# Splitting attention-projection weights one chunk ahead, and both ScalarE writes of a turned head pair first

## The chip, the cores and the metric

The kernel runs on one core of a Trainium2 chip. The metric is the device time of one execution in microseconds (us): the median of several runs. Beside the runs there is one profiled execution, whose trace shows every instruction. The engines are TensorE (PE, with its weight loads PEld), VectorE (DVE), ScalarE (ACT), GpSimd (POOL) and the sync engine (SP), which here only issues transfers.

## The reference

Two layers of an encoder on a sequence of 512 positions with 1024 channels. Each layer is a half-step feed-forward block, a mixer, and another half-step feed-forward block, all with an RMS norm and an adaptive shift, scale and gate in front. The change touches only the mixer, and of it the projections to the queries, keys and values of two attentions:

```python
def hybrid_mixer(h, w_in, qk_gain, rel_bias, forget_bias, w_pool, pool_scale, w_branch, w_out):
    proj = h @ w_in
    qa, ka, va, ub, qc, kc, vc, f_lin, g_lin = jnp.split(proj, SPLIT_POINTS, axis=-1)
    ya = chunked_relpos_attention(ha(qa), ha(ka), ha(va), qk_gain[0], qk_gain[1], rel_bias)
    yb = multiscale_pool(ub, w_pool, pool_scale)
    yc = forgetting_attention(hc(qc), hc(kc), hc(vc), qk_gain[2], qk_gain[3], f_lin + forget_bias)
    ...
    branch = jnp.einsum('bsnw,nwd->bsnd', ys, w_branch)
    gates = jax.nn.sigmoid(g_lin.reshape(B, S, N_BRANCHES, D_MODEL))
    merged = jnp.sum(gates * branch, axis=2)
    return merged @ w_out
```

Both attentions have 8 heads of 64 channels. Their queries and keys are RMS-normed per head and scaled by a gain; logits get a bias, then softmax, then the product with the values.

## The kernel before

All products keep close to fp32 precision by a split: a number x becomes hi, its value in the rounded type fp32r, and lo = x - hi. A product of x and y is then three TensorE products, hi by hi, hi by lo and lo by hi. `triple` (lines 137 to 142) issues these three; its lines 139 to 141 are where most of TensorE's time stands.

**Weight chunks.** `wchunk` (lines 296 to 312) brings in 128x1024 weights: a transfer on the sync queue into a tile `raw` (line 300; two places), a ScalarE copy that rounds it to hi (line 309), and a VectorE subtraction that makes lo (line 311). hi and lo lie in one place of the tag `w`, of which there are three. A chunk can be brought in when a place of `raw` and one of `w` are free, that is when VectorE has made the lo of the second chunk before, and TensorE has done the products of the chunk that held the place.

**Projections.** Queries, keys and values of the two attentions are six columns of 512 channels, numbered 0 to 5 (`col`). `proj` (lines 780 to 819) makes one column for all 512 positions, in four accumulators `acc` of 128 positions each. Its weights come in four chunks c = 0 to 3 of 256 input rows. Chunks 0 and 1 are used one after the other: bring it in, then 8 triples over 2 row blocks (`kk`) and 4 position blocks (`t`). Chunks 2 and 3 are then brought in together and held, and each `t` in turn gets its last 4 triples and is evacuated. Column 0 of a layer has its own path, with its first three chunks brought in during the phase before. `proj` is a generator: it gives way after each triple.

For queries and keys (`proj_qk`, lines 838 to 906) the evacuation copies the accumulator (line 846), squares it on ScalarE (line 848) and sums per head on VectorE (line 849). Later come eight small steps for the norm, and four **turns** (lines 869 to 889). A turn takes a pair of heads: four TensorE transposes into one PSUM tile `pt` (line 872), and then, for each of the two heads, which lie in partitions 0 to 63 and 64 to 127:

- a ScalarE write of the scaled, rounded half (line 881);
- for queries a transfer, issued by GpSimd, that copies it to the other half of the partitions (line 884), and a GpSimd memset (line 885);
- a VectorE step that computes the remainder lo (line 887).

**Where they run.** `Mixer.run` (lines 1171 to 1260) first makes columns 0 and 1, the forget gates (`forget`, lines 921 to 952) and column 2. Then comes `attention` of group a (lines 984 to 1074) on columns 0 to 2. For each head and each block of 128 positions it issues the logits (lines 995, 996), the minimum of the negated logits on VectorE (line 999), the exponential on ScalarE (line 1003), and the division by the sum on GpSimd or VectorE (line 1007). The blocks' transposes (line 1019) with their split (lines 1023, 1024), and the product with the values (lines 1041 to 1048), come later, by a list of tasks with due times counted in TensorE work (`later`, `poll`; one unit is a product of 512 columns, and LAG_T = 30 units lie between a block's logits and its transposes). Between the blocks a filler generator gets 9 units of products each. The filler of group a is columns 3, 4 and 5 (`fill_a`, lines 1187 to 1190); that of group c is the gates and branch products of the merge.

**Order.** The code lists the instructions, but it doesn't fix their order on an engine: the program is laid out at build time by readiness, in which earlier code goes first among what is ready, and by explicit rules where the code gives one. On the chip every engine works through its own list in that order.

Of the kernel before, what the change touches and what calls it, by code (L numbers as in the profile page):

```python
# [18 lines left out]
AF = mybir.ActivationFunctionType  # L19
# [21 lines left out]
def encoder_kernel(tc, xT, c, w_ada, b_ada, gains, w_gate, w_up, w_down, w_qkv, w_f, w_ubg,  # L41
                   qk_gain, rel, fbias, w_pool, pool_scale, w_branch, w_out, inv_cnt, w_first, out):
    nc = tc.nc
# [252 lines left out]
    def wchunk(src, shape, side=True, spare=None, lo_eng=None, place=WIDE):  # L296
        lo_eng = lo_eng or nc.vector
        side_work(side)
        raw = st([P] + list(shape), F32, *(("b", NB) if spare else ("raw", NRAW)))
        last["dma"] = nc.sync.dma_start(raw, src).ins  # L300
        if spare == "ptb":
            hi, lo = duo(shape, "ptb")
        elif spare == "b":
            hi = st([P] + list(shape), F32R, "b", NB)
            lo = st([P] + list(shape), F32R, "b", NB)
        else:
            hi, lo = duo(shape, "w", place)
        with behind("scalar"):
            nc.scalar.copy(hi, raw)  # L309
        with behind("vector"):  # L310
            lo_eng.tensor_tensor(lo, raw, hi.bitcast(F32), op=ALU.subtract)  # L311
        return hi, lo
# [463 lines left out]
    def qkv_chunk(l, col, c, **kw):  # L776
        return wchunk(w_qkv[l, 2 * c * P:(2 * c + 2) * P, col * T:(col + 1) * T]
                      .rearrange("(k p) c -> p k c", p=P), (2, T), **kw)

    def proj(l, col, evac, pre=None, norm=None):  # L780
        accs = [acc() for _ in range(NT)]

        def three(t, k, hi, lo):
            tk = slice(t * P, (t + 1) * P)
            triple2(accs[t], hhi[:, k, tk], hlo[:, k, tk], hi, lo, k == 0, k == KD - 1)

        if norm is not None:
            for hs in range(2):
                norm.back(hs, mmt)
                if hs == 0:  # L790
                    later(FRONT2, lambda: norm.front(1, mmt))
                    later(BACK2, lambda: norm.back(1, mmt))
                both = (2 * hs, 2 * hs + 1)
                for k in range(6):
                    hi, lo = pre[k // 2]
                    for t in both:
                        three(t, k, hi[:, k % 2, :], lo[:, k % 2, :])
                if hs == 0:
                    rest = qkv_chunk(l, col, 3)
                for t in both:  # L800
                    for kk in range(2):
                        three(t, 6 + kk, rest[0][:, kk, :], rest[1][:, kk, :])
                    evac(t, accs[t])
                yield
            return
        else:
            for c in range(2):
                hi, lo = qkv_chunk(l, col, c)
                for kk in range(2):
                    for t in range(NT):  # L810
                        three(t, 2 * c + kk, hi[:, kk, :], lo[:, kk, :])
                        yield
        held = [(c, *qkv_chunk(l, col, c)) for c in (2, 3)]
        for t in range(NT):
            for c, hi, lo in held:
                for kk in range(2):
                    three(t, 2 * c + kk, hi[:, kk, :], lo[:, kk, :])
                    yield
            evac(t, accs[t])

    def triple2(o, lh, ll, rh, rl, start, stop):
        triple(o, lh, ll, rh, rl, start, stop)
# [15 lines left out]
    def proj_qk(l, col, gcol, is_q, res, pre=None, norm=None):  # L838
        lows = []
        qs = []  # L840

        def evac(t, a):
            if t == 0:
                qs.extend((st([P, NT, T], F32, "ptb", 2), st([P, NT, H], F32, "qss", 1)))
            qn, ss = qs
            nc.scalar.copy(qn[:, t, :], a)
            sq = t2(T)
            nc.scalar.activation(sq, a, AF.Square)  # L848
            nc.vector.tensor_reduce(ss[:, t, :], sq.rearrange("p (h d) -> p h d", h=H), axis=AX.X, op=ALU.add)

        yield from proj(l, col, evac, pre, norm)
        qn, ss = qs
        norm_of = {}

        def first():
            v = st([P, NT * H], F32, "nt_v32", 2)
            nc.vector.tensor_scalar(v, ss.rearrange("p t h -> p (t h)"), 1.0 / HD, EPS, op0=ALU.mult, op1=ALU.add)
            norm_of["steps"] = rsqrt_steps(v, NT * H)
            next(norm_of["steps"])

        def step():
            norm_of["r"] = next(norm_of["steps"])

        def scale(t):
            q3 = qn[:, t, :].rearrange("p (h d) -> p h d", h=H)
            r = norm_of["r"][:, t * H:(t + 1) * H].unsqueeze(2).to_broadcast([P, H, HD])
            nc.vector.tensor_tensor(q3, q3, r, op=ALU.mult)

        def turn(p):
            pt = mmt()  # L870
            for t in range(NT):
                nc.tensor.transpose(pt[:, t * P:(t + 1) * P], qn[:, t, p * P:(p + 1) * P], ident)
            pe[0] += 2.2
            b = blk("b")
            if is_q:
                lows.append(blk("b"))
            first, second = slice(0, HD), slice(HD, P)
            for odd, (own, other) in enumerate(((first, second), (second, first))):
                dst = b[:, odd, :]
                gc = gcol[own, :]  # L880
                nc.scalar.activation(dst[own, :], pt[own, :], AF.Identity, scale=gc)
                low = dst[other, :]
                if is_q:
                    nc.gpsimd.dma_start(low.bitcast(F32), dst[own, :].bitcast(F32))
                    nc.gpsimd.memset(lows[p][other, odd, :].bitcast(F32), 0.0)
                    low = lows[p][own, odd, :]
                nc.vector.scalar_tensor_tensor(low, pt[own, :], gc, dst[own, :].bitcast(F32),
                                               op0=ALU.mult, op1=ALU.subtract)
            res.append((b, lows[p]) if is_q else b)

        todo = [first, step, step, step] + [lambda t=t: scale(t) for t in range(NT)]
        todo += [lambda p=p: turn(p) for p in range(4)]
        turns.append(todo)
        for n in range(8):
            later(PACE * n, lambda n=n: todo.pop(0)() if len(todo) == 12 - n else None)

        def ready(p):
            if len(todo) >= 4 - p:
                if heads[0] < (Q_GATE if is_q else K_GATE)[p]:
                    later(8, lambda: ready(p))  # L900
                else:
                    while len(todo) >= 4 - p:
                        todo.pop(0)()

        for p in range(4):
            later(TURN + 12 * p, lambda p=p: ready(p))
# [423 lines left out]
```

## Time and profile before

| | |
|---|---|
| runs, median (lowest to highest) | 2371.16 us (2369.97 to 2371.98) |
| the profiled execution | 2367.45 us |
| its span, first to last instruction | 2365.7 us |
| TensorE clock granted | 1.000 of full speed |
| DMA, mean over the span | 137 GB/s |

The span is one execution's; a sum of terms is made against it and then carried over to the median. "Idle before" is the time in which an engine had nothing running before an instruction, and the releaser is what ended it, read from the semaphores. Matmuls overlap, so a busy TensorE is one that always had the next product ready, and its idle time is what other engines cost it.

### The profile page before, as it was taken

The page shows a single profiled execution, that of the slowest core. Times are in us where ns is not written, and L with a number is a line of the kernel's source. Part 1 is how long each engine was busy: PE and PEld are TensorE (multiplying, and loading weights), DVE is VectorE, ACT ScalarE, POOL GpSimd, SP SyncE. Part 2 cuts the span into 40 slices and gives each one's busy share as a digit, 9 for nine tenths or more (in the row PEclk, how much of TensorE's full clock was granted, in tenths as well). Part 3 has the DMA queues.
Part 4 walks back from the last instruction along what each step waited for, and adds up shares of the span by engine and source line. Part 5 has one row for each costly group of instructions (what it writes and reads, how often), then busy time and mean ns, then how long its engine had stood idle before and what let it go on. Part 6 is the DMA issues. An engine that isn't in the chain of part 4 may idle for free.

```text
span 2365.7 us, 37435 instructions
## 1 busy us (share of the span) xinstructions
PE 2336.6 (99%) x14322; PEld 2077.1 (88%) x14322; DVE 1771.6 (75%) x3147; ACT 1198.3 (51%) x2097; POOL 325.8 (14%) x433
## 2 busy tenths in 40 slices
PE   7999999999999999999999999999999999999999
PEld 5898998878888898989999989978888888999898
DVE  8887866787686577878687878677866855878583
ACT  5353555676632363635553536456765324636262
POOL 3000011244411110000100000112443211000000
PEclk9999999999999999999999999999999999999999
DMA  8535342333355524353425353533333654143333
GB/s 294 180 107 187 101 167 88 106 98 110 120 196 208 187 72 160 115 181 106 152 63 178 99 186 108 187 107 99 98 122 106 216 205 167 63 143 108 100 99 105
DMA packets 117976, 325.16 MB, mean 137 GB/s; under 512 B 11651, under 2 KB 13827, under 8 KB 117797
## 3 DMA queue, kind: packets, MB, share of 16 engines
q1 hardware_dynamic: 115106, 314.38, 40.1%
q0 software_dynamic: 2688, 8.39, 1.2%
q8 instruction: 112, 1.84, 0.3%
q14 instruction: 68, 0.55, 0.1%
q10 hardware_dynamic: 2, 0.00, 0.0%
HBM read 312.16 MB, written 6.38 MB: 135 GB/s over the span
## 4 chain that ended last, share of the span: by engine, by line
PE 89%; DVE 6%; ACT 2%; DMA 1%; issue 1%; POOL 0%; SPq 0%; ACTq 0%; DVEq 0%; POOLq 0%
PE acc L139 16%; PE acc L141 16%; PE acc L140 16%; PE acc L148 5%; PE mm L149 5%; PE mm L150 5%; PE mm L148 5%; PE acc L149 5%; PE acc L150 5%; PE mm L141 3%; PE mm L139 3%; PE mm L140 3%; PE mm L1019 1%; DVE v L226 1%; DVE w L311 1%
## 5 line engine op out<-in xcount | busy, mean ns | idle before, releaser
L311 DVE TENSOR_TENSOR w<-raw,w 128x1024 fp32r<-128x1024 f32 x247 | 313.0, 1271 | 163.8 <-ACT w L309 163.6
L309 ACT CAST w<-raw 128x1024 fp32r<-128x1024 f32 (+1 forms) x255 | 264.4, 1041 | 275.5 <-PE acc L141 191.4
L139 PE MATMUL acc<-b,w 128*128 128x512 f32 (+1 forms) x960 | 359.8, 375 | 0.0
L141 PE MATMUL acc<-b,w 128*128 128x512 f32 (+1 forms) x960 | 356.3, 371 | 0.0
L140 PE MATMUL acc<-b,w 128*128 128x512 f32 (+1 forms) x960 | 356.3, 371 | 0.0
L141 PEld LDWEIGHTS acc<-b,w 128*128 128x128 f32 x960 | 180.3, 188 | 31.8
L139 PEld LDWEIGHTS acc<-b,w 128*128 128x128 f32 x960 | 180.3, 188 | 30.1
L140 PEld LDWEIGHTS acc<-b,w 128*128 128x128 f32 x960 | 180.4, 188 | 29.8
L416 ACT CAST ptb<-v 128x1024 fp32r<-128x1024 f32 x140 | 147.0, 1053 | 97.1 <-DVE v L485 58.2
L417 DVE TENSOR_TENSOR ptb<-v,ptb 128x1024 fp32r<-128x1024 f32 x140 | 170.8, 1223 | 32.6 <-ACT ptb L416 27.6
L139 PE MATMUL acc<-hhi,w 128*128 128x512 f32 x480 | 191.8, 401 | 2.6 <-ACT hhi L746 1.7
L141 PE MATMUL acc<-hhi,w 128*128 128x512 f32 x480 | 188.4, 393 | 1.8 <-DVE w L311 1.8
L140 PE MATMUL acc<-hlo,w 128*128 128x512 f32 x480 | 188.2, 392 | 1.1 <-DVE hlo L749 1.1
L416 ACT CAST w<-raw 128x1024 fp32r<-128x1024 f32 (+1 forms) x140 | 116.5, 832 | 120.7 <-PE acc L141 56.0
L417 DVE TENSOR_TENSOR w<-raw,w 128x1024 fp32r<-128x1024 f32 (+1 forms) x140 | 133.4, 953 | 13.2 <-ACT w L416 13.2
L139 PE MATMUL acc<-w,hhi 128*128 128x512 f32 x336 | 138.8, 414 | 0.8 <-ACT t L848 0.8
L140 PE MATMUL acc<-w,hhi 128*128 128x512 f32 x336 | 131.7, 392 | 0.0
L141 PE MATMUL acc<-w,hlo 128*128 128x512 f32 x336 | 131.7, 392 | 0.0
L226 DVE CUSTOM_DVE_ANT_0 v<-v,b,badac 128x1024 f32<-128x1024 f32 x87 | 116.7, 1351 | 11.6 <-DMA v<-in_w_ada_dram 11.3
L466 DVE SCALAR_TENSOR_TENSOR xv<-acc,badac,xv 128x512 f32<-128x512 f32 (+1 forms) x112 | 77.4, 691 | 54.8 <-PE acc L141 54.7
L148 PE MATMUL acc<-b,ptb 128*128 128x256 f32 x420 | 117.3, 279 | 0.0
L149 PE MATMUL mm<-b,ptb 128*128 128x256 f32 x420 | 117.3, 279 | 0.0
(312 smaller groups left out, 6619.4 us busy)
## 6 DMA issues: line engine op xcount, KB each, us to landing
raw<-in_w_down_dram SPq DMA_DIRECT2D x88, 512.0 KB, 4.0
v<-in_w_ada_dram SPq DMA_DIRECT2D x87, 512.0 KB, 5.1
raw<-in_w_up_dram SPq DMA_DIRECT2D x82, 512.0 KB, 3.6
raw<-in_w_gate_dram SPq DMA_DIRECT2D x79, 512.0 KB, 3.6
b<-in_w_ada_dram SPq DMA_DIRECT2D x57, 512.0 KB, 4.7
raw<-in_w_ubg_dram SPq DMA_DIRECT2D x56, 512.0 KB, 3.6
raw<-in_w_qkv_dram SPq DMA_DIRECT2D x42, 512.0 KB, 3.8
raw<-in_w_branch_dram SPq DMA_DIRECT2D x24, 512.0 KB, 3.6
```

The costliest lines, as they stand in the source:

```text
L139: mm(o, lh, rh, start=start, stop=False)
L140: mm(o, lh, rl, start=False, stop=False)
L141: mm(o, ll, rh, start=False, stop=stop)
L148: mm(o, lh, rh, start=start and k == 0, stop=False, skip_group_check=True)
L149: mm(o, lh, rl, start=False, stop=False, skip_group_check=True)
L150: mm(o, ll, rh, start=False, stop=k == 3, skip_group_check=True)
L226: dot = nc.vector.tensor_tensor_reduce(out=raw, in0=raw, in1=silc[0], scale=1.0, scalar=badac[:, l, j, d:d + 1], op0=ALU.mult, op1=ALU.add ...
L309: nc.scalar.copy(hi, raw)
L311: lo_eng.tensor_tensor(lo, raw, hi.bitcast(F32), op=ALU.subtract)
L416: nc.scalar.copy(hi, src)
L417: nc.vector.tensor_tensor(lo, src, hi.bitcast(F32), op=ALU.subtract)
L466: nc.vector.scalar_tensor_tensor(x, acc_j, gate, x, op0=ALU.mult, op1=ALU.add)
```

## The change

Two independent edits. In `proj`, a chunk is brought in before the products of the chunk ahead of it are issued, not after them; and the first chunk of the next column is brought in at the middle of a column's last part (`t == 2`), and handed over in a dictionary `next_chunk`. Column 0 doesn't take part, and column 5 has no next. Chunk 3 keeps its place. In a turn, the two ScalarE writes are issued first, and then transfer, memset and VectorE remainder of the one and of the other head.

```diff
         else:
+            ready = next_chunk.pop((l, col), None) or qkv_chunk(l, col, 0)
             for c in range(2):
-                hi, lo = qkv_chunk(l, col, c)
+                (hi, lo), ready = ready, qkv_chunk(l, col, c + 1)
                 for kk in range(2):
                     for t in range(NT):
                         three(t, 2 * c + kk, hi[:, kk, :], lo[:, kk, :])
                         yield
-        held = [(c, *qkv_chunk(l, col, c)) for c in (2, 3)]
+        held = [(2, *ready), (3, *qkv_chunk(l, col, 3))]
         for t in range(NT):
+            if t == 2 and col < 5:
+                next_chunk[l, col + 1] = qkv_chunk(l, col + 1, 0)
             for c, hi, lo in held:
                 for kk in range(2):
                     three(t, 2 * c + kk, hi[:, kk, :], lo[:, kk, :])
                     yield
             evac(t, accs[t])
+
+    next_chunk = {}
...
             first, second = slice(0, HD), slice(HD, P)
-            for odd, (own, other) in enumerate(((first, second), (second, first))):
+            sides = ((first, second), (second, first))
+            for odd, (own, other) in enumerate(sides):
+                nc.scalar.activation(b[own, odd, :], pt[own, :], AF.Identity, scale=gcol[own, :])
+            for odd, (own, other) in enumerate(sides):
                 dst = b[:, odd, :]
                 gc = gcol[own, :]
-                nc.scalar.activation(dst[own, :], pt[own, :], AF.Identity, scale=gc)
                 low = dst[other, :]
                 if is_q:
                     nc.gpsimd.dma_start(low.bitcast(F32), dst[own, :].bitcast(F32))
```

## The prediction

> **What bounds the kernel now.** I read the page's totals and its chain of waits first, then TensorE's list of waits, then the busy time by stretch, and last the order of time around the places that these name.
>
> ```profile
> span 2365.7 us, 37435 instructions
> PE 2336.6 (99%) x14322; PEld 2077.1 (88%) x14322; DVE 1771.6 (75%) x3147; ACT 1198.3 (51%) x2097; POOL 325.8 (14%) x433
> PE 89%; DVE 6%; ACT 2%; DMA 1%; issue 1%; POOL 0%; SPq 0%; ACTq 0%; DVEq 0%; POOLq 0%
> ```
>
> TensorE works in 99% of the span and has 89% of the chain that ended last. An edit that adds or removes no matrix product can only win back TensorE's waits. The changed code runs in two stretches of each layer: the first three columns of projections (395 to 445 us, 1563 to 1613), and attention of group a, whose filler is columns 3 to 5 (445 to 545, 1613 to 1713). After it comes attention of group c, whose filler is gate products.
>
> ```profile
> core 0: us, PE busy (x) PEld busy (x) DVE busy (x) ACT busy (x) POOL busy (x), PEclk, DMA share, GB/s
> 395.00:445.00 50.00, 50.00 (x237) 40.02 (x236) 39.54 (x73) 30.13 (x44) 7.86 (x17) 1.00 0.43 122
> 445.00:545.00 100.00, 97.66 (x534) 81.51 (x533) 79.06 (x215) 71.76 (x169) 43.05 (x62) 1.00 0.32 94
> 545.00:650.00 105.00, 103.66 (x565) 87.14 (x564) 72.07 (x187) 69.76 (x164) 47.39 (x75) 1.00 0.38 118
> 1563.00:1613.00 50.00, 50.00 (x237) 40.02 (x236) 39.65 (x74) 30.11 (x45) 7.86 (x17) 1.00 0.43 122
> 1613.00:1713.00 100.00, 97.67 (x534) 81.55 (x533) 78.87 (x214) 71.82 (x167) 43.10 (x62) 1.00 0.33 94
> ```
>
> Columns: the stretch, its length, then busy time of each engine. In the first three columns TensorE is busy for 50.00 of 50.00 us, in both layers: nothing is to be won there. In attention of group a it idles for 2.34 and 2.33 us. These 4.67 us are the whole idle time of the stages that change, 0.20% of the kernel. Who ended them stands in the list of waits (total, times, longest):
>
> ```profile
> PE mm L1019 <- DVE b L887: 2.4, 2, 1.2
> PE mm L872 <- DVE mx L999: 1.0, 2, 0.5
> PE acc L139 <- ACT t L848: 0.8, 2, 0.4
> PE mm L872 <- DVE pta L1024: 0.5, 2, 0.2
> ```
>
> 2.4 + 1.0 + 0.8 + 0.5 = 4.7 us, each once a layer: the attention's and the turns' own small steps. None is a product waiting for its weight chunk. The groups of the projections' products say the same (after the bar: busy, mean ns, idle before and who ended it):
>
> ```profile
> L139 PE MATMUL acc<-w,hhi 128*128 128x512 f32 x336 | 138.8, 414 | 0.8 <-ACT t L848 0.8
> L140 PE MATMUL acc<-w,hhi 128*128 128x512 f32 x336 | 131.7, 392 | 0.0
> L141 PE MATMUL acc<-w,hlo 128*128 128x512 f32 x336 | 131.7, 392 | 0.0
> ```
>
> The second product of a triple reads the chunk's lo, the last thing made of it, and it waited 0.0 us in 336 cases.
>
> **The change part by part. The chunks.** No instruction is added or taken away. For three of a column's four chunks (c = 0, 1, 2; the fourth keeps its place) one transfer, one ScalarE copy (L309, 1.04 us in the row below) and one VectorE subtraction (L311, 1.33 us below) stand earlier in the code by one chunk of products: 8 triples of 3 products, 24 x 0.227 = 5.4 us of TensorE. (0.227 us is the spacing of starts: 523.55, 523.78, 524.01 below.)
>
> ```profile
> 523.55 0.39 PE L139 MATMUL acc<-w,hhi 128*128 128x512 f32 x1
> 523.78 0.40 PE L140 MATMUL acc<-w,hhi 128*128 128x512 f32 x1
> 524.01 0.40 PE L141 MATMUL acc<-w,hlo 128*128 128x512 f32 x1
> ```
>
> What they save directly is 0, by the groups above. Nor is the place in the code the place in the queue:
>
> ```profile
> 417.26 1.04 ACT L309 CAST w<-raw 128x1024 fp32r<-128x1024 f32 x1
> 418.19 0.58 ACT L846 COPY ptb<-acc 128x512 f32<-128x512 f32 x1
> 421.67 0.58 ACT L934 COPY t<-mm 8x512 f32<-8x512 f32 x1 [0.48 <-PE mm L931]
> ```
>
> The copy at 417.26 is for the first chunk of column 2 (the forget gates' product at L934, which has only a small split of its own, stands before it in the code, and so does the last evacuation of column 1 at 418.19). So the order in which the program was laid out already draws splits ahead of earlier code, as far as a place is free. With three places for w, of which a column's last part holds two, there is one to run ahead with, before and after the change.
>
> What does move is where these steps of ScalarE and VectorE fall among the attention's steps. In the attention stretch VectorE is busy 79% and ScalarE 72%, and neither lets a short step pass a long one. The place where this is paid now:
>
> ```profile
> 488.61 1.33 DVE L311 TENSOR_TENSOR w<-raw,w 128x1024 fp32r<-128x1024 f32 x1
> 489.48 0.68 ACT L881 ACTIVATE b<-mm,qg 64x512 fp32r<-64x512 f32 x1
> 489.94 0.27 DVE L1024 TENSOR_TENSOR pta<-mm,pta 128x128 fp32r<-128x128 f32 x1
> 490.20 0.74 DVE L887 SCALAR_TENSOR_TENSOR b<-mm,qg,b 64x512 fp32r<-64x512 f32 x1
> 490.26 0.66 PE L872 MATMUL mm<-ident,ptb 128*128 128x128 f32 x4 [0.23 <-DVE pta L1024]
> 490.98 0.68 ACT L881 ACTIVATE b<-mm,qg 64x512 fp32r<-64x512 f32 x1 [0.81 <-DVE b L887]
> 491.68 0.37 ACT L1045 COPY yl<-mm 64x256 f32<-64x256 f32 x1
> 491.69 0.76 DVE L887 SCALAR_TENSOR_TENSOR b<-mm,qg,b 64x512 fp32r<-64x512 f32 x1 [0.75 <-ACT b L881]
> 492.48 0.42 DVE L1046 TENSOR_TENSOR yl<-mm,yl 64x256 f32<-64x256 f32 x1
> 492.60 0.41 PE L1019 MATMUL mm<-ident,t 128*128 128x128 f32 x2 [1.21 <-DVE b L887]
> ```
>
> A chunk's subtraction (488.61, 1.33 us) is followed by L1024 and the turn's L887, for which TensorE then waits 0.23 and 1.21 us. If the subtraction goes elsewhere, at most 0.23 + 1.21 = 1.44 us a layer, 2.9 in both, is won. It then stands in front of other steps; nine chunks a layer are moved in this stretch, and the like wait can arise anew, so the other bound is +2.9 us. I take -1.0, a third of the gain: nothing says that the new place is worse than this one, and VectorE has 21 us idle in the stretch to hold it.
>
> Behind the moved transfers the sync queue carries the attention's bias strips. A strip is used by VectorE's L999, and TensorE's wait on L999 is 1.0 us in all, quoted above; the strip itself ends no wait of TensorE, so I cost this at 0 (1.0 us if that cover went).
>
> **The turns.** The rows above also show a turn as it is: ScalarE write (489.48), VectorE remainder (490.20), second ScalarE write (490.98, held 0.81 us for the first remainder), second remainder (491.69 to 492.45). From 489.48 to 492.45 are 2.97 us. How often ScalarE is held so:
>
> ```profile
> L881 ACT ACTIVATE b<-mm,qg x32: 681/683/687, 406.9 to 1678.7; 64x512 fp32r<-64x512 f32 x32
> L887 DVE SCALAR_TENSOR_TENSOR b<-mm,qg,b x32: 735/747/759, 407.6 to 1679.5; 64x512 fp32r<-64x512 f32 x32
>   DVE b L887: 13.6, 14
> ```
>
> The second write reads the other half of the same PSUM tile as the first remainder and does not touch its output, yet it waits for it in 14 of 32 turns, 13.6 us. Readers of one PSUM tile are kept apart by the program, so with the new order I expect the hold the other way: the first remainder waits for the second write. One engine's next step starts 0.1 us before the last one's end (417.26 + 1.04 = 418.30 against 418.19, above), and the handover to the other engine takes 0.04 (490.20 + 0.74 = 490.94 against 490.98). The chain is then 0.68 + 0.68 + 0.75 + 0.75 - 0.2 + 0.04 = 2.70: 0.27 us shorter, once a layer where TensorE waits for it: -0.5. The bounds: at best both waits on L887 go, -2.4 (shared with the 2.9 above, not on top of it: 1.21 of each 1.44 is the same wait). At worst the first remainder starts 0.6 us later and holds VectorE; behind it stand L1046 and the next L999, for which ScalarE's L1047 and L1003 wait, then TensorE's transposes: 0.6 at the two places without cover is +1.2. The fills of the key's other half that GpSimd issues (L884) stand on its queue in the old order, and the second of them is ready sooner; their logits come a head later, so 0.
>
> The Trainium skill ("PSUM — Partial Sum Buffer", PSUM bank collisions raise a hardware error) says that two engines may use one bank at once if their partitions lie in different groups of 32, which these halves do. This case's trace shows the two held apart all the same (0.81 us at 490.98). If the new program let them overlap, the sum would have some 0.5 us less a turn; I go by the trace.
>
> **The sum.** -1.0 - 0.5 = -1.5 us on the profiled span of 2365.7, that is 2364.2. That execution took 2367.45 us, 3.7 under the median of the runs, 2371.16, so I carry the difference over to the median: 2369.7 us.
>
> **The rivals.** *All waits go.* Splits a chunk early leave VectorE free when the short steps come. The four waits above go, -4.7, and so does the idle time of the next stretch (105.00 - 103.66 = 1.34 a layer, 2.7), which begins in whatever order the last chunks leave: 2371.2 - 7.4 = 2363.8. For it: in two of the four waits a long step of VectorE stands just ahead. Against it: the evacuation L848 and the turn's scaling cause the others, and these don't move.
>
> *A slot wait takes their place (slower).* The second chunk of a column is now issued before the products of the first. Its place is free only after the previous column's held products. Where ScalarE's queue reaches that copy early, it stands still, and the exponentials and evacuations behind it are late. Such waits exist:
>
> ```profile
> 399.66 1.05 ACT L309 CAST w<-raw 128x1024 fp32r<-128x1024 f32 x1 [3.42 <-PE acc L141]
> 405.10 1.05 ACT L309 CAST w<-raw 128x1024 fp32r<-128x1024 f32 x1 [4.39 <-PE acc L141]
> ```
>
> There they cost nothing, since no attention stands behind them. In attention a block's transposes come 30 units, 30 x 0.227 = 6.8 us, after its logits. The steps between (L999, L1003, L1007) take some 2.8 us if no queue holds them, so 4 us of hold are covered at best, and none where TensorE waits already. From that point it decides: of 4.4 us between 0.4 and 4.4 come through, at three column starts a layer. With 1.5 each, 6 x 1.5 = +9: 2380. Against it: the last evacuation of a column stands in the same queue and waits for still later products.
>
> *Nothing moves.* If the laid-out order is already bound by the three places, both kernels split at the same moments, and the time stays at 2371.2.
>
> **How the numbers follow.** My forecast has 0.33, nothing moves 0.17, all waits go 0.22, the slot wait 0.28. A difference of 0.2%, 4.7 us, is about what a measurement of this kernel can tell from no change (its three runs lie 2.0 us apart). The first two cases fall within it, so 0.50; faster 0.22, slower 0.28. The likeliest case's own range, from its bounds of -2.9 to +4.1 (2.9 + 1.2), is 2368.3 to 2375.3; with the rivals on both sides I give 2363.5 to 2381.
>
> **What would show it.** Right: ScalarE's second write of a turn follows its first within 0.1 us, and its waits for the remainder are gone; TensorE's idle time in attention of group a stays between 1 and 4 us a layer; the projections' products still wait 0.0 for their chunks. Wrong: copies of chunks that wait for TensorE inside attention with exponentials behind them (the slot wait), or idle time under 0.5 us a layer (all waits go). A change in the feed-forward stages would mean that the laid-out order shifted beyond the code that was edited, which I have not costed.

## The result and the profile after

The changed kernel takes 2375.24 us (median of 20 runs, 2372.57 to 2379.43), the kernel before 2370.73 (median of 20 runs beside them, 2367.59 to 2373.53). The ratio is 1.0019, 95% interval 1.0013 to 1.0025: 4.5 us slower. The number lies in the range given, at its upper half; the forecast of 1.5 us faster has the wrong sign.

The page of the changed kernel first: span, busy time by engine, and the chain that ended last.

```profile
span 2373.7 us, 37467 instructions
PE 2340.2 (99%) x14322; PEld 2076.6 (87%) x14322; DVE 1770.9 (75%) x3147; ACT 1198.4 (50%) x2097; POOL 326.8 (14%) x433
PE 89%; DVE 5%; ACT 3%; issue 1%; DMA 1%; SPq 0%; ACTq 0%; DVEq 0%
```

The work is the same: 14322 products, 3147 steps of VectorE, 2097 of ScalarE, with the same busy time within 1 us on both. The profiled execution is 2375.45 us. Next the busy time by stretch: the first three columns, then attention of group a in both layers, cut at the same first and last product as in the kernel before.

```profile
core 0: us, PE busy (x) PEld busy (x) DVE busy (x) ACT busy (x) POOL busy (x), PEclk, DMA share, GB/s
396.44:446.44 50.00, 50.00 (x237) 40.02 (x236) 39.59 (x73) 29.98 (x44) 7.87 (x17) 1.00 0.43 122
...
446.66:549.17 102.51, 98.94 (x533) 81.36 (x532) 80.05 (x217) 72.93 (x170) 43.53 (x62) 1.00 0.32 94
1617.71:1720.14 102.43, 98.87 (x533) 81.35 (x532) 79.57 (x216) 72.81 (x170) 43.79 (x62) 1.00 0.32 93
```

The first three columns still have no idle TensorE. Attention of group a, 100.0 us long before, is now 102.5 and 102.4: this is where the kernel lost, some 2.5 us in each layer. Only half of it shows as idle time (102.51 - 98.94 = 3.57, against 2.34 before). The other half shows as busy time of the same products (98.94 against 97.66), because a product's modelled length of 0.39 us is longer than the usual 0.227 between two starts: a gap up to 0.16 us hides in it. A busy TensorE is therefore not always one that had its next product ready, and the experiments below are compared by starts of products, not by idle time.

TensorE's list of waits (total, times, longest), the rows of this stage:

```profile
PE mm L1026 <- DVE b L894: 2.8, 2, 1.4
...
PE mm L877 <- DVE mx L1006: 1.0, 2, 0.5
PE acc L139 <- ACT t L853: 0.9, 2, 0.5
PE mm L1048 <- DVE pta L1031: 0.7, 2, 0.3
PE mm L1049 <- DVE ptb L1031: 0.5, 2, 0.3
...
PE mm L877 <- DVE pta L1031: 0.5, 2, 0.2
PE mm L1049 <- DVE pta L1031: 0.4, 2, 0.2
```

(The lines have moved: L885 is the turn's ScalarE write, L894 its VectorE remainder, L877 its transposes; L1026 the attention's transposes, L1030 and L1031 their split, L1048 and L1049 the value products, L1006, L1010, L1012 and L1014 the minimum, exponential, reciprocal and division.) The four waits of before are all still there, within 0.4 us. New are three rows at the value products, 0.7 + 0.5 + 0.4 = 1.6 us, all ended by the split L1031 on VectorE. The reason stands one view further, the turn's own steps: who ended the idle time before the remainder, here of the changed kernel,

```profile
L894 DVE SCALAR_TENSOR_TENSOR b<-mm,qg,b x32: 737/750/759, 409.8 to 1684.6; 64x512 fp32r<-64x512 f32 x32
...
its engine sat idle before it (us, times) until:
  ACT b L885: 16.5, 28
```

and the same row of the kernel before:

```profile
  ACT b L881: 9.8, 12
```

ScalarE's 14 holds of 13.6 us are gone, as the edit meant. VectorE's have gone from 12 to 28, and they stand in another place: before, 10 of the 12 came ahead of the second remainder, which waited for its own write; now all 28 come ahead of the first remainder, which waits for the write of the other half. Over all 32 turns of the two traces, the second write follows the first within 0.03 us in 28 (none before); a turn, from the start of the first write to the end of the second remainder, takes 3.19 us on average (3.56 before); and the first remainder starts 0.95 us after the end of its own write (0.38 before). **The turn became 0.4 us shorter, and VectorE starts on it 0.6 us later.**

What that does stands in the order of time, at the place that the prediction showed. The changed kernel is 1.42 us behind here (the chunk's subtraction starts at 490.03, before at 488.61):

```profile
490.03 1.34 DVE L311 TENSOR_TENSOR w<-raw,w 128x1024 fp32r<-128x1024 f32 x1
490.91 1.39 ACT L885 ACTIVATE b<-mm,qg 64x512 fp32r<-64x512 f32 x2
492.33 1.51 DVE L894 SCALAR_TENSOR_TENSOR b<-mm,qg,b 64x512 fp32r<-64x512 f32 x2 [0.70 <-ACT b L885]
492.72 0.68 ACT L885 ACTIVATE b<-mm,qg 64x512 fp32r<-64x512 f32 x1
493.88 0.42 DVE L1053 TENSOR_TENSOR yl<-mm,yl 64x256 f32<-64x256 f32 x1
494.33 0.41 ACT L1054 CAST b<-yl 64x256 fp32r<-64x256 f32 x1 [0.93 <-DVE yl L1053]
494.76 0.68 ACT L885 ACTIVATE b<-mm,qg 64x512 fp32r<-64x512 f32 x1
495.48 0.74 DVE L894 SCALAR_TENSOR_TENSOR b<-mm,qg,b 64x512 fp32r<-64x512 f32 x1 [0.58 <-ACT b L885]
496.31 0.37 ACT L1030 CAST pta<-mm 128x256 fp32r<-128x256 f32 x1
496.51 0.76 DVE L894 SCALAR_TENSOR_TENSOR b<-mm,qg,b 64x512 fp32r<-64x512 f32 x1
497.30 0.83 DVE L1014 TENSOR_SCALAR t<-t,rs 128x512 f32<-128x512 f32 x1
498.17 0.42 DVE L1031 TENSOR_TENSOR pta<-mm,pta 128x256 fp32r<-128x256 f32 x1
498.64 0.39 PE L1048 MATMUL mm<-pta,xv 128*128 128x256 f32 x1 [0.34 <-DVE pta L1031]
```

and the rows of the kernel before that answer to its second half:

```profile
493.24 0.36 ACT L1023 CAST pta<-mm 128x256 fp32r<-128x256 f32 x1
493.43 0.74 DVE L887 SCALAR_TENSOR_TENSOR b<-mm,qg,b 64x512 fp32r<-64x512 f32 x1
494.09 0.40 DVE L1024 TENSOR_TENSOR pta<-mm,pta 128x256 fp32r<-128x256 f32 x1
494.38 0.68 ACT L881 ACTIVATE b<-mm,qg 64x512 fp32r<-64x512 f32 x1
495.12 0.76 DVE L887 SCALAR_TENSOR_TENSOR b<-mm,qg,b 64x512 fp32r<-64x512 f32 x1
```

In the first turn both writes run back to back from 490.91, and VectorE, ready at 491.6, stands idle for 0.70 us until the second write has ended. In the second turn a step of ScalarE that itself waits for VectorE (494.33) has come between the writes, so the first remainder, whose own write had ended at 493.40 (492.72 + 0.68), starts at 495.48, with VectorE idle for the last 0.58 us. In the kernel before, the attention's split passed between the two halves of this turn: its copy (493.24) ran on ScalarE ahead of the second write (494.38), which had to let the first remainder go first, and its subtraction (494.09) on VectorE between the two remainders (493.43 and 495.12). Now its copy stands behind the second write and its subtraction behind both remainders and the division: 496.31 and 498.17, that is 1.65 and 2.66 us later when the 1.42 are taken off, and TensorE waits at 498.64 where it didn't before. What passed through ScalarE's hold now stands behind the step that was held.

The key turns show the same in another place of the changed kernel:

```profile
531.76 0.76 DVE L894 SCALAR_TENSOR_TENSOR b<-mm,qkgc,b 64x512 fp32r<-64x512 f32 x1
...
532.16 0.39 PE L141 MATMUL acc<-w,hlo 128*128 128x512 f32 x1
532.54 0.69 DVE L1031 TENSOR_TENSOR ptb<-mm,ptb 128x512 fp32r<-128x512 f32 x1
532.66 0.36 PE L1048 MATMUL mm<-ptb,xv 128*128 128x256 f32 x1
...
533.29 0.39 PE L1049 MATMUL mm<-ptb,xv 128*128 128x256 f32 x1 [0.28 <-DVE ptb L1031]
```

The split at 532.54 has stood behind a remainder (it ends at 532.52), and the value products at 532.66 and 533.29 start late: the first 0.50 us after the start of L141, where 0.227 is usual, the second with 0.28 us of idle time.

The starts of TensorE's products, compared one by one between the two traces, tell where the whole loss arises; layer 2 repeats layer 1 within 0.02 us. Around the query turns 0.19 us are lost at the transposes behind the first turn, 0.30 at the logits at 497.37 and 0.66 at the value products at 498.64. Around the key turns 0.89 are lost at the value products at 532.66 and 533.29, and 0.38 at the logits at 540.12. The rows of the changed kernel that aren't shown above:

```profile
493.99 0.41 PE L1026 MATMUL mm<-ident,t 128*128 128x128 f32 x2 [1.41 <-DVE b L894]
494.16 0.48 PE L140 MATMUL acc<-w,hhi 128*128 128x512 f32 x1
...
496.77 0.48 PE L139 MATMUL acc<-w,hhi 128*128 128x512 f32 x1
497.37 0.30 PE L1002 MATMUL mm<-b,b 128*128 128x128 f32 x1
...
539.22 0.76 DVE L894 SCALAR_TENSOR_TENSOR b<-mm,qkgc,b 64x512 fp32r<-64x512 f32 x1
539.59 0.39 PE L141 MATMUL acc<-w,hlo 128*128 128x512 f32 x1
540.12 0.35 PE L1002 MATMUL mm<-b,b 128*128 128x256 f32 x1
```

The logits at 540.12 start 0.14 us after a remainder has ended (539.98), and its semaphore is the last that they wait for. Those at 497.37 start 0.10 us after the second remainder has ended (497.27), though the profile names no releaser there. Logits, turned blocks and value products share the four places of one PSUM tag (`mm`), so a block that VectorE reads late can hold back a product that doesn't use it; this reason is read from the program, the times from the trace. Of the 0.89 us, 0.27 stand at the first value product, which also waits for a remainder, and the rest at the split. At the transposes the laid-out order has changed: a product that ran ahead of them before (L140, at 491.00) now stands behind them (494.16). So in each layer some 1.3 us belong to the late split, 0.95 to late remainders and 0.2 to the moved product; of their sum 0.1 comes back by the end of the key stretch.

The profiled span is 8.0 us longer, more than the medians differ. Between the same products, attention of group a with the stretch behind it has 5.07 us of it in the two layers (table below). The rest lies in the start (1.4 us by 395 us, of which a kernel with the order of before shows 0.8 too) and in stretches of the merge and feed-forward, which differ by 1 to 2 us from one trace to the next.

### The profile page after: what moved, and what is told of

It is laid out like the page before. It is cut to its first block, busy times and chain, and to the rows that moved or that the text cites. A ratio compares the mean times of both kernels' runs of the same rounds, so it can differ in the third digit from the quotient of the medians.

```text
span 2373.7 us, 37467 instructions
## 1 busy us (share of the span) xinstructions
PE 2340.2 (99%) x14322; PEld 2076.6 (87%) x14322; DVE 1770.9 (75%) x3147; ACT 1198.4 (50%) x2097; POOL 326.8 (14%) x433
## 4 chain that ended last, share of the span: by engine, by line
PE 89%; DVE 5%; ACT 3%; issue 1%; DMA 1%; SPq 0%; ACTq 0%; DVEq 0%
PE acc L139 16%; PE acc L141 16%; PE acc L140 16%; PE acc L148 5%; PE mm L149 5%; PE mm L150 5%; PE mm L148 5%; PE acc L149 5%; PE acc L150 5%; PE mm L141 3%; PE mm L139 3%; PE mm L140 3%; PE mm L1026 1%; DVE v L226 1%; PE mm L1049 1%
## 5 line engine op out<-in xcount | busy, mean ns | idle before, releaser
L141 PE MATMUL acc<-b,w 128*128 128x512 f32 (+1 forms) x960 | 356.3, 371 | 0.0
L140 PE MATMUL acc<-b,w 128*128 128x512 f32 (+1 forms) x960 | 356.3, 371 | 0.0
L141 PEld LDWEIGHTS acc<-b,w 128*128 128x128 f32 x960 | 180.3, 188 | 31.7
L140 PEld LDWEIGHTS acc<-b,w 128*128 128x128 f32 x960 | 180.4, 188 | 29.9
L141 PE MATMUL acc<-hhi,w 128*128 128x512 f32 x480 | 188.7, 393 | 2.2 <-DVE w L311 2.2
L140 PE MATMUL acc<-hlo,w 128*128 128x512 f32 x480 | 188.3, 392 | 2.0 <-DVE hlo L749 2.0
L140 PE MATMUL acc<-w,hhi 128*128 128x512 f32 x336 | 132.0, 393 | 0.0
L141 PE MATMUL acc<-w,hlo 128*128 128x512 f32 x336 | 131.5, 391 | 0.0
```

The source lines that it names most:

```text
L140: mm(o, lh, rl, start=False, stop=False)
L141: mm(o, ll, rh, start=False, stop=stop)
```

## The experiments

Sixteen kernels, each timed in 5 rounds against the kernel before on the same chip, whose median was 2369.12 to 2370.49 us in the five groups. Beside the ratio a second measure is used: the time between the same products of TensorE, counted in its order, in four stretches of each layer. "Start" is the first three columns but for their beginning, with all turns of group a, and the first products of attention (396.7 to 454.4 us in the trace of before); "query" holds the first three query turns of group c (to 504.7), "key" the fourth and three of the key turns (to 555.6), "next" the last key turn and what follows (to 610.4). The numbers are differences to the kernel before, layer 1 / layer 2, in us:

| kernel | median | ratio, 95% interval | start | query | key | next | sum of both layers |
|---|---|---|---|---|---|---|---|
| the change | 2375.24 | 1.0019 (1.0013 to 1.0025) | 0.00 / 0.00 | 1.15 / 1.17 | 1.16 / 1.24 | 0.18 / 0.17 | 5.1 |
| chunks_only | 2368.56 | 0.9997 (0.9988 to 1.0006) | 0.01 / 0.04 | 0.01 / -0.04 | -0.11 / 0.17 | 0.00 / 0.01 | 0.1 |
| turns_only | 2375.3 | 1.0023 (1.0014 to 1.0032) | 0.00 / 0.00 | 1.15 / 1.18 | 1.08 / 1.18 | 0.18 / 0.18 | 5.0 |
| turns_q | 2371.61 | 1.0009 (1.0 to 1.0018) | 0.05 / 0.04 | 1.07 / 1.72 | -0.11 / 0.21 | 0.00 / 0.00 | 3.0 |
| turns_k | 2371.41 | 1.0008 (0.9999 to 1.0017) | 0.01 / -0.01 | 0.01 / 0.02 | 1.05 / 1.19 | 0.18 / 0.20 | 2.7 |
| sbuf_old | 2378.37 | 1.0036 (1.0022 to 1.005) | 0.01 / -0.01 | 1.11 / 2.62 | 1.55 / 1.68 | 0.00 / 0.00 | 7.0 |
| sbuf_new | 2379.68 | 1.0042 (1.003 to 1.0055) | 0.01 / -0.01 | 1.09 / 2.67 | 1.58 / 1.67 | 0.00 / 0.00 | 7.0 |
| twice_old | 2381.25 | 1.0048 (1.0036 to 1.0061) | 2.53 / 3.95 | 0.99 / 1.04 | 1.62 / 1.90 | 0.00 / 0.01 | 12.0 |
| twice_new | 2379.68 | 1.0043 (1.0031 to 1.0056) | 1.73 / 1.67 | 1.16 / 1.17 | 2.17 / 2.18 | -0.01 / 0.02 | 10.1 |
| prec60_old | 2373.83 | 1.0016 (1.0007 to 1.0025) | 0.89 / 0.88 | -0.59 / -0.55 | 0.88 / 0.99 | 0.00 / 0.01 | 2.5 |
| prec60_new | 2375.38 | 1.0026 (1.0016 to 1.0035) | 0.85 / 0.83 | -0.61 / -0.58 | 2.45 / 2.57 | -0.28 / -0.27 | 5.0 |
| prec_old | 2373.67 | 1.0016 (1.0007 to 1.0025) | 0.84 / 0.83 | 0.11 / 0.15 | 0.69 / 0.81 | -0.01 / 0.01 | 3.4 |
| prec_new | 2376.25 | 1.0028 (1.0017 to 1.0038) | 0.84 / 0.84 | 0.25 / 0.34 | 2.45 / 2.59 | -0.28 / -0.27 | 6.8 |
| split_prec_old | 2369.59 | 0.9999 (0.999 to 1.0008) | 0.05 / 0.04 | -0.51 / -0.51 | 0.04 / 0.15 | -0.01 / 0.01 | -0.7 |
| split_prec_new | 2372.89 | 1.0011 (1.0002 to 1.002) | -0.01 / 0.00 | 0.39 / 0.44 | 0.87 / 0.98 | -0.01 / 0.00 | 2.7 |
| vec_second | 2379.92 | 1.0046 (1.0032 to 1.0059) | 1.88 / 1.88 | 1.17 / 1.23 | 0.27 / 0.38 | 0.00 / 0.01 | 6.8 |
| rem_twice | 2374.77 | 1.0026 (1.0016 to 1.0036) | 0.87 / 0.85 | 0.73 / 0.74 | 0.91 / 0.91 | 0.00 / 0.00 | 5.0 |

**Which part costs.** chunks_only has the edit of `proj` alone, turns_only that of the turn alone; turns_q and turns_k have the turn's new order for the queries or the keys alone, with `both = not is_q` in turns_k:

```diff
+            both = is_q
+            if both:
+                for odd, (own, other) in enumerate(sides):
+                    nc.scalar.activation(b[own, odd, :], pt[own, :], AF.Identity, scale=gcol[own, :])
             for odd, (own, other) in enumerate(sides):
...
+                if not both:
+                    nc.scalar.activation(dst[own, :], pt[own, :], AF.Identity, scale=gc)
```

> Theory A (the turns cost it): with the chunk edit alone nothing moves on any engine, since the laid-out order already had the splits that early; ratio to the kernel before 1.000 within 0.0005, TensorE idle in attention of group a 2.3 us a layer as before. Theory B (the moved chunks cost it): ratio about 1.0019, idle in that stretch up by about 2 us a layer.

> Theory A: the whole change, ratio about 1.0019 (4.5 us), VectorE held 28 times for the second ScalarE write of a turn, 16 us in all. Theory B: ratio 1.000 or a little under, since ScalarE's 14 holds (13.6 us) go.

> New order of writes in the turns of the queries alone. Theory A, if all turns inside attention cost alike: about half of 4.5 us, ratio 1.0010. If only the turns cost in which GpSimd must also fill the other half: all of it, 1.0019.

> New order in the turns of the keys alone. Theory A, if all turns cost alike: ratio 1.0010. If the cost hangs on the queries' fills: 1.000.

The chunk edit does nothing: 0.9997, and no stretch moves by more than 0.2 us. Attention of group a in the busy time by stretch, and two rows of TensorE's waits, both of chunks_only:

```profile
446.05:546.08 100.03, 97.66 (x534) 81.50 (x532) 79.16 (x216) 71.80 (x168) 43.20 (x62) 1.00 0.33 95
```

```profile
PE mm L1024 <- DVE b L892: 2.4, 2, 1.2
PE mm L877 <- DVE mx L1004: 1.0, 2, 0.5
```

These are the numbers of before. The reason is in the program itself: in the traces, the order of instructions on each of the five engines is the same with the chunk edit as without it, and the order of the whole change is the same as that of the turn edit alone. The whole difference is the turn's, 1.0023, and its two halves, 1.0009 and 1.0008, add up to it within their intervals, each with its 1.1 to 1.7 us in its own stretch. By time alone neither half is clear of noise, since both intervals reach 1.000; it is the stretches that tell them apart.

**Is it the shared PSUM tile?** Here ScalarE first copies the turned block from PSUM to SBUF (into the columns of `qn` that were just transposed), and the writes and remainders read the copy; once with the old code order, once with the new.

```diff
+            pc = qn[:, :, p * P:(p + 1) * P]
+            nc.scalar.copy(pc, pt.rearrange("p (t c) -> p t c", t=NT))
...
-                nc.scalar.activation(dst[own, :], pt[own, :], AF.Identity, scale=gc)
+                nc.scalar.activation(dst[own, :].rearrange("p (t c) -> p t c", t=NT), pc[own], AF.Identity, scale=gc)
...
-                nc.vector.scalar_tensor_tensor(low, pt[own, :], gc, dst[own, :].bitcast(F32),
+                nc.vector.scalar_tensor_tensor(low.rearrange("p (t c) -> p t c", t=NT), pc[own], gc, dst[own, :].bitcast(F32).rearrange("p (t c) -> p t c", t=NT),
```

> ScalarE first copies the turned pair from PSUM to SBUF (one more step of about 0.6 us a turn); writes and remainders then read the copy, in the old code order. Theory H (the cost is VectorE's hold on a PSUM tile that ScalarE still reads): no remainder waits for the second write any more, the PSUM tile is free after the copy, TensorE's 1.2 us wait for it at the first query turn shrinks; ratio to the kernel before between 0.998 and 1.001. Theory S (the cost is that ScalarE's writes stand back to back and its short steps come late): a third step in a row makes it worse, ratio 1.002 or more.

> The same copy with the new code order of the writes. Theory H: the hold was all that the order decided, so the time is that of the old order with the copy, within 0.0005. Theory S: about 0.002 above it.

With the copy the order in the code makes no difference: 1.0036 and 1.0042, intervals that overlap, stretches equal within 0.05 us, and in the two traces every engine has the same order. In the trace of sbuf_new the second write follows the first within 0.03 us in 28 of 32 turns, as in the changed kernel, but the first remainder starts 0.15 us after its own write on average, where the changed kernel has 0.95. So the order acts through the tile in PSUM that both engines read, and through nothing else. What the hold costs, these two kernels don't tell: theory H had 0.998 to 1.001 for sbuf_old and was missed, and the 1.0036 is as theory S had it, because of the copy's own load or because the writes stand back to back here too. VectorE still stands idle before the first remainder, 26 times and 15.6 us in sbuf_new, now for that remainder's own write; its idle time alone is thus no measure of the hold. As a remedy the copy is no use: it costs 8 to 10 us by the ratios, with a wait of TensorE that ends with the copy (L875), in sbuf_old:

```profile
PE mm L1043 <- ACT ptb L875: 2.8, 2, 1.4
```

**Is it the length of the hold?** The second ScalarE write is issued twice, in both orders. In the new order VectorE's first remainder waits for both.

```diff
                 nc.scalar.activation(dst[own, :], pt[own, :], AF.Identity, scale=gc)
+                if odd:
+                    nc.scalar.activation(dst[own, :], pt[own, :], AF.Identity, scale=gc)
```

> Old order, second ScalarE write of each turn issued twice. Theory H: the second remainder alone comes 0.7 us later; ratio 1.000 to 1.002. Theory S: ScalarE does 0.7 us more a turn in a row, ratio 1.002.

> New order, second write issued twice: both remainders come another 0.7 us later. Theory H: about twice the cost of the change, ratio 1.004, and VectorE's holds for ScalarE in turns grow from 16 us to over 25. Theory S: ratio like that of the old order with the write twice, plus at most 0.002.

Both cost about the same, 1.0048 and 1.0043, and much of it lies in the start stretch, which the change itself leaves alone (2.53 and 3.95 us in twice_old): there an accumulator waits for the evacuation of column 2's values, for which the list of waits of before has no row. In twice_old:

```profile
PE acc L139 <- DVE xv L417: 4.6, 2, 2.3
```

The dose that should have told the new order from the old is drowned by what 0.68 us more on ScalarE do anyway. The pair is inconclusive on the hold: what both theories had for the old order (at most 1.002) was missed, and VectorE's idle time before the remainders of twice_new is 15.2 us in 21 holds, not the 25 that theory H asked for; the 1.0043 fits both theories. It does show that more of ScalarE's time in a turn is paid in either order.

**Can the attention's short steps be let past?** The steps between the logits and the value products get precedence when the program is laid out: in prec60 as if they stood 60 instructions earlier, in prec without a limit, and in split_prec (60) the split of the transposed block alone.

```diff
-            nc.scalar.copy(dh, tv)
-            nc.vector.tensor_tensor(dl, tv, dh.bitcast(F32), op=ALU.subtract)
+            with tc.high_priority(60):
+                nc.scalar.copy(dh, tv)
+                nc.vector.tensor_tensor(dl, tv, dh.bitcast(F32), op=ALU.subtract)
```

(In prec60 and prec the same stands around the minimum, exponential, reciprocal and division, and around the steps behind the value products.)

> New order of writes; the attention's short steps (minimum, exponential, reciprocal, division, the splits of transposes, the evacuation of the value products) get precedence over code up to 60 instructions ahead of them. Theory P (the old order's hold kept a turn's steps apart and let these short steps pass between them; the new order sends the turn ahead in one piece): the cost of the change goes, ratio to the kernel before 0.999 to 1.0005, and the split of a transposed block no longer stands behind both remainders. Theory H (the first remainder comes 0.7 us later, whatever passes): still 0.002 above the old order with the same precedence.

> Old order with the same precedence. Theory P: 0.998 to 1.000, and the new order is within 0.0007 of it. Theory H: 0.998 to 1.000, and the new order 0.002 above.

> New order; the same steps have precedence over all other code. Theory P: 0.999 to 1.0005, unless turns and splits now come late in their place (then above 1.001, with TensorE waiting for chunks or for the turns). Theory H: 0.002 above the old order with it.

> Old order with precedence over all other code. Theory P: like the new order with it, within 0.0007. Theory H: 0.002 under it.

> New order of writes; of the attention's short steps only the split of transposed blocks (one ScalarE copy, one VectorE subtraction) has precedence over code up to 60 instructions ahead. Theory P (what the new order costs is that this split comes behind both remainders of a turn): TensorE's 1.15 us more in the stretch of the query turns and its 0.9 us more in that of the key turns go, in each layer; whole kernel 0.9985 to 1.0003. Theory H (the hold of the first remainder costs by itself): both stay, 1.002. Theory O (any shift of these queues costs; nothing singles out the split): 1.001 to 1.003, with the waits at other steps.

> Old order with the same precedence. Theory P: within 0.0007 of the new order with it. Theory H: 0.002 under it. Theory O: 1.000 to 1.002, in no relation to it.

No theory's numbers came true for the whole kernel: with precedence for all short steps the new order is 0.0010 to 0.0012 above the old, between P (0.0007) and H (0.002), and all four kernels are slower than before. By stretches it is clearer. In prec60 the query stretch is shorter than before by the same 0.6 us in both orders: there the turn's new order costs nothing as soon as the short steps don't queue behind it. (In prec, without a limit, the two orders differ by 0.14 to 0.19 us there.) In the key stretch the new order still costs 1.6 us more than the old (2.45 against 0.88), by a wait that is in the list of neither prec60_old nor the changed kernel: the transposes of a turn for the turn's own scaling, which has come late. In prec60_new:

```profile
PE mm L872 <- DVE ptb L867: 2.6, 2, 1.3
PE mm L1022 <- DVE b L889: 2.4, 2, 1.2
```

Precedence for the split alone is cheap and bears on its share: the new order with it costs 2.7 us in the stretches, without it 5.0; but the old order gains 0.7 by it too, so by these kernels the split accounts for 5.0 - (2.7 + 0.7) = 1.6 of the 5.0 us, less than the 2.6 read from the places above. In time it is 1.0011 against 1.0023, with intervals that overlap. Theory P, by which the cost should have gone (0.9985 to 1.0003), was missed, and the ratio is one that theory O named (1.001 to 1.003). With the split out of the way the logits wait for the remainder, in split_prec_new:

```profile
PE mm L997 <- DVE b L889: 1.0, 2, 0.5
```

That any shift costs, as theory O has it, doesn't hold: the old order's query stretch became 0.5 us shorter with the same precedence. split_prec_old is the best of the six kernels with precedence and no better than the kernel before, 0.9999 (0.999 to 1.0008).

**Which engine's lateness is it?** One rival was left: that not VectorE's hold but ScalarE's two writes in a row delay its own short steps. vec_second has the old order and lets VectorE make the second write, which takes work from ScalarE; rem_twice has the old order and issues the first remainder twice, which leaves ScalarE's work as it is.

```diff
 vec_second:
-                nc.scalar.activation(dst[own, :], pt[own, :], AF.Identity, scale=gc)
+                if odd:
+                    nc.vector.tensor_scalar(dst[own, :], pt[own, :], gc, None, op0=ALU.mult)
+                else:
+                    nc.scalar.activation(dst[own, :], pt[own, :], AF.Identity, scale=gc)
 rem_twice:
                 nc.vector.scalar_tensor_tensor(low, pt[own, :], gc, dst[own, :].bitcast(F32),
                                                op0=ALU.mult, op1=ALU.subtract)
+                if not odd:
+                    nc.vector.scalar_tensor_tensor(low, pt[own, :], gc, dst[own, :].bitcast(F32),
+                                                   op0=ALU.mult, op1=ALU.subtract)
```

> Old code order, but the second write of a turn is made by VectorE (0.74 us there in place of 0.68 us on ScalarE); no handover back to ScalarE is left in a turn. Theory S (TensorE pays for ScalarE steps in a row): the stretch of the query turns falls under that of the kernel before by 0.3 to 1 us a layer, ratio 0.9985 to 1.0003. Theory V (it pays for VectorE's remainders and splits being late, whoever makes them late): 32 turns load VectorE by 0.74 us each, the stretch is 1 us or more above before, ratio 1.0015 or more.

> Old code order, first remainder of a turn issued twice: VectorE has 0.75 us more a turn and the second write and remainder come that much later, ScalarE's load is unchanged. Theory S: little, ratio under 1.0010. Theory V: like the second ScalarE write issued twice in the old order, 1.003 to 1.005, with the query stretch 1 us or more up.

Both are slower, 1.0046 and 1.0026. In rem_twice VectorE hardly stands still for the writes any more (its idle time before the remainders, the row that has 9.8 and 12 in the kernel before), and yet TensorE waits in new places:

```profile
  ACT b L881: 1.6, 6
```

```profile
PE mm L1022 <- DVE yl L1049: 2.1, 2, 1.0
...
PE acc L139 <- DVE xv L417: 1.6, 2, 0.8
...
PE mm L998 <- DVE mx L1002: 1.5, 2, 0.7
```

All three are ended by VectorE. So 0.75 us more of VectorE's time in a turn are paid with 0.7 to 0.9 us a stretch, and the work taken from ScalarE in vec_second doesn't make up for it. vec_second is as theory V had it; rem_twice stays under V's numbers (1.003, and 1 us in the query stretch) and over S's 1.0010. That lateness of VectorE is enough for a loss of this size is shown; rem_twice also loses 0.9 us in the start stretch, where the change loses nothing. That ScalarE's part is nil is not shown for the whole, since twice_old charges ScalarE alone and is slower as well. At the two late splits it can be read: ScalarE's copies had ended 1.49 us before the subtraction at 498.17 (496.31 + 0.37 = 496.68) and 0.96 us before the one at 532.54, so there the subtraction stood in VectorE's queue and didn't wait for the copy.

What stays open: how much of the loss is the hold on the chip, and how much the order in which the program was laid out around it. No kernel here lets VectorE read one half of the PSUM tile while ScalarE reads the other, so the wait alone has no price.

## Why the prediction was wrong, point by point

**The bound held.** TensorE's waits for the attention's and the turns' small steps were named as all that the edits can change, the projections' products as waiting for no chunk. The difference lies in this stage, and the first three columns are still full. But the waits of before bound a gain, not a loss: most of the loss arose at logits and value products that hadn't waited.

**The chunks, -1.0 us: the term fell.** Measured are +0.1 us in the eight stretches and 0.9997 in time. The prediction's sentence that the layout already draws splits ahead of earlier code as far as a place is free was right, and it should have ended the argument there: *nothing moves*, a rival at 0.17, is what the chunk edit does, to the last instruction of each engine. The bounds of ±2.9 were about steps that never moved. The slot wait and *all waits go* fall with it.

**The turns, mechanism right, size wrong.** Forecast was that the hold turns round, that the second write follows the first within 0.1 us (28 of 32 turns), that ScalarE's waits vanish (13.6 us to none) and that the chain gets shorter by 0.27 us; over all turns it became shorter by 0.37 (3.56 to 3.19). Forecast as the bad end was that the first remainder starts 0.6 us later; it does, 0.38 to 0.95 on average. The three signs named for being right came, the first in 28 of 32 turns (TensorE's idle time in the stage is 3.57 and 3.56 us a layer, and the projections' products still wait 0.0 us for their chunks), but they would have come with a gain too: they tell that the hold turned, not what it costs. The step that failed is the pricing of that: "0.6 at the two places without cover is +1.2", set as a bound, with -0.5 taken. It measured +5.0 us (turns_only), four times the bound. Two reasons. The hold was priced only where TensorE waits already, though it now comes in 28 turns. The 14 in the first three columns cost nothing (0.00 in the start stretch); of the others, most in a stage where VectorE is busy 79%, what stands behind them had less cover than the delay at the logits and value products of 497.37, 498.64, 532.66, 533.29 and 540.12. And the prediction saw ScalarE's hold as pure loss. It was a gap through which short steps passed: the split's copy on ScalarE, and its subtraction between the two remainders on VectorE, which came 2.66 us later once the gap had closed.

**The gain had no taker.** -0.5 was credited because the chain ends in a remainder for which TensorE waits (1.2 us before). At that place the chain is 0.04 us shorter (492.33 + 1.51 - 490.91 = 2.93 against 2.97), and TensorE's wait is 1.4. The 0.2 us of overlap in the sum were read from steps on different tiles; here the two writes take 1.39 us together and the two remainders 1.51, so within a turn nothing overlaps.

The Trainium skill's statement ("PSUM — Partial Sum Buffer", PSUM bank collisions raise a hardware error) that two engines may read one bank at once in different groups of 32 partitions was set aside in favour of the trace, and the trace of the changed kernel agrees with that choice: VectorE was held 28 times, 16.5 us in all, for a write that reads the other 64 partitions. The statement itself is neither confirmed nor refuted, since in no kernel do the two read one PSUM tile at the same time.

**The range** held the time by luck: it reached to 2381 for the slot wait, a mechanism that did not occur; the forecast's own range, to 2375.3, ended where the measurement came out.

## What to carry to other kernels

When two engines take turns on one tile, the order of their steps decides not whether but which of them stands still. Here it was cheaper on ScalarE, busy 72% of the stage, than on VectorE, busy 79%, though one case doesn't show that the less busy engine is always the better choice. Look at what short steps used to pass through the old hold. Price a hold by everything queued behind it on that engine and by the places that its tile keeps, also where nothing waits today: here such a hold cost four times what the two visible waits suggested. And before costing a moved step, compare the laid-out order of each engine with that of before: if it is the same, the edit is nothing.

## What the runs showed of the hardware that was not expected

The time between two products of TensorE in a stage bound by it repeats far better than the whole: 57.62 and 57.63 us, 50.34 and 50.35, 54.81 and 54.81 between the kernel before and chunks_only, which have the same order (in layer 1; within 0.04 in layer 2), and within 0.02 us in the first, second and fourth stretch between the changed kernel and turns_only. The key stretch repeats less well, by 0.06 to 0.17 us in the same pairs. In the same pairs the profiled executions start up to 0.8 us apart by the same product, and the times of 20 runs spread over 6 to 7 us. A cost of 1 us in a known stretch is thus plain in one trace each, where single runs spread by more than the 4.5 us that the medians of 20 tell.
